# Order of ScalarE's and VectorE's work in the heads of a hybrid decoder block: recurrence work queued behind the takes, weight splits written one product ahead

## The chip, the cores and the metric

The kernel runs on one core of a Trainium2 chip. The metric is the device time of one execution in microseconds (us), as the median of several executions. Before the change it is 1460.81 us (3 runs, 1459.44 to 1462.52).

## The reference

One layer of a decoder block on x of 1024 tokens by 1024 channels, all in float32. Cut to what matters:

```python
proj = x @ w_in                       # 1024 x 7168
q, f_pre, i_val, o_gate, pool_v, gate_a, gate_b = jnp.split(proj, splits, axis=-1)
qf = silu(q) * 128 ** -0.5
f = lb + (1.0 - lb) * sigmoid(f_pre)
k = 1.0 - f
# per head (8 heads of 128): S_t = diag(f_t) S_{t-1} + k_t v_t^T ; o_t = S_t^T q_t
o = hgrn2_chunked(qf, k, i_val, log(f))
o = o * rsqrt(mean(o * o, -1) + 1e-6)             # per head
a = (o * hgrn_norm_g * sigmoid(o_gate)) @ w_a
pooled = causal_multiscale_pool(pool_v)           # trailing means over 2, 4, 8, 16 tokens, minus the token
b = per_group(pooled @ w_pool) * pool_scale
mix = (sigmoid(gate_a) * a + sigmoid(gate_b) * b) @ w_out
x = layer_norm(alpha * x + mix)
x = layer_norm(alpha * x + square(relu(x @ w_up)) @ w_down)
```

## The kernel before, in words

**Products.** A float32 product is made of three float32r matmuls: each operand is split into a high part (a cast on ScalarE, L126 for weights, L131 for activations) and a low part (the rest, a subtraction on VectorE, L127 and L132), and high x high, high x low and low x high are summed in one PSUM bank (`prod`, L212, L214, L215: 12 matmuls of 128x128 by 128x512 for a contraction of 512). A large product is a 2 by 2 block scheme with seven products in place of eight (`pair`, L267): seven weight operands, four of them blocks and three sums of blocks (`make_t3` L284, `make_t2` L301, `t4` L309, `t1` L316, on VectorE), and seven products p1 to p7. Their results are drained by copies on ScalarE (`copied`, L275) and sums on VectorE (`added`, L279), and handed to a "take", which is what this place in the kernel does with the result (a sigmoid, a store). Here these drains and takes together are called takes.

**The heads.** After the value projection (to about 115 us) come 24 such pairs one after the other: inputs of the heads (q and f), output gates, pooled values, gates a and b (`ORDER`, `POOL_AFTER`, L33 to L38). Each pair loads its raw weight blocks on SyncE's DMA queue (`loaded_blocks`, L231). `run` (L379) writes, for each of the seven steps, the weight operand (sum and split), then the product with its takes, and then one "turn" of what goes beside it. In this part TensorE's instructions keep the order in which they are written (`manual_schedule`); the other engines' instructions are put in order by a scheduler which goes by priority (the order of writing, with takes up by 60) and by its own estimate of when things are ready. Each engine then works through its queue in that order, and an instruction that has to wait holds up what stands behind it.

**Beside the products.** `recurrence` (L1046) gives the turns: 16 halves (8 heads by 2 halves of the tokens), 8.25 turns each. A half's `prepare` (L890) makes the scaled queries and keys: scans on VectorE (L897, L901, L905), k = 1 - f on ScalarE (L909), products on VectorE (L935 to L956) and copies of half tiles on ScalarE (L940, L943, L953, L955). `scores`, `far_queries`, `states` and `outputs` follow; `outputs` (L1019) squares the output on ScalarE (L1031), takes the root (L1032, with the load of another activation table), its reciprocal on VectorE (L1033), and scales the output by it in four ScalarE instructions (L1035), all in one turn. In the last two pairs (gates 6 and 7) the turns are those of `pool_products` (L746): weights and pooled rows are loaded, split (L126, L127) and multiplied (`mm3`, L113 to L115), and each result is multiplied on VectorE by a gate that is loaded again from DRAM (`loaded(gbd...)`, L784, L791) into a ring of four tiles, and stored (L792). The last two results are only scaled, on ScalarE (L789).

**What follows.** `o_operand` (L628) loads four tiles of the heads' outputs (L635) and splits them (L131, L132) for the products with w_a; "a11" is the first of seven such operands (L1167). Then come the products with w_a (`a_pair`, L1142; their takes load gates and pooled rows again, L1129, L1130), w_out, the norms and the MLP.

Of the kernel before, what the change touches and what calls it, by code (L numbers as in the profile page):

```python
# [29 lines left out]
PER_HALF = 8.25  # L30
TURN_BACK = 4
TURNS_AHEAD = 3
ORDER = (  # L33
# [18 lines left out]
def tile_hybrid_block(  # L52
# [189 lines left out]
    def w_tile():  # L242
        return wq.tile([P, CH, P], F32R, tag="w", name=nm("w"), bufs=NW)

    def w_part(src):
        return split(src, w_tile)

# [19 lines left out]
    def pair(raw, rooms, takes, pz_tag="pj", twin=False, pc_tag="pj", turned=False):  # L267
# [5 lines left out]
        def copied(room, ps):  # L273
            t = room()
            A.copy(t, ps)  # L275
            return t
# [377 lines left out]
    with tc.tile_pool(name="tmp", bufs=1, side="right", reuse_waits="tile") as tmp:  # L654
# [25 lines left out]
        def head_inputs(h, behind=()):  # L680
            fs, qs = inputs[h] = [None, None], [None, None]

            def room_f():
                fs[1] = tt("f")
                return fs[1]

            def take_f(u):
                def take(src):
                    t = fs[u] = fs[u] or tt("f")
                    A.activation(t, src, AF.Sigmoid)  # L690
                    A.activation(t, t, AF.Identity, bias=lb[:, h : h + 1], scale=one_lb[:, h : h + 1])
                return take

            def take_q(u):
                def take(src):
                    t = qs[u] = tt("q")
                    A.activation(t, src, AF.Sigmoid)
# [5 lines left out]
            run(pair(  # L703
                blocks, (c_soon, c_late, room_f),
                (take_q(0), take_f(0), take_q(1), take_f(1)),
            ), behind=behind)

# [4 lines left out]
        def output_gates(h):  # L712

            def take(dst, src=False):
                def put(t):
                    s = c_late() if src else t
                    A.activation(s, t, AF.Sigmoid)
                    nc.sync.dma_start(out=dst, in_=s)
                return put

            run(pair(
                loaded_blocks(w_in, 3 * D + h * P, 3 * D + (h + 1) * P), (c_soon, c_late, c_late),
                (take(ogd[h][0]), take(ogd[h + 1][0], True), take(ogd[h][1]), take(ogd[h + 1][1])),
            ))

        def gates(j):
# [3 lines left out]
            def take(dst, src=None, u=None):  # L730
                def put(t):
                    s = (tt("og") if final else c_late()) if src else t
                    A.activation(s, t, AF.Sigmoid)
# [5 lines left out]
            run(pair(  # L739
                loaded_blocks(w_in, 5 * D + j * P, 6 * D + j * P), (room if final else c_soon, room, room),  # L740
                (take(gad[j][0]), take(gbd[j][0], True, 0), take(gad[j][1]), take(gbd[j][1], False, 1)),
            ))

        held = [None, None]

        def pool_products():  # L746
# [29 lines left out]
            for n, (g, u) in enumerate(todo):  # L776
# [28 lines left out]
        def pooled(g):  # L805
# [49 lines left out]
            def take_12(ps):  # L855
# [5 lines left out]

            run(pair(
                loaded_blocks(w_in, 4 * D + j * P, 4 * D + (j + 1) * P),
# [21 lines left out]
        class Half:  # L885
# [4 lines left out]
            def prepare(self):  # L890
# [16 lines left out]
                )  # L907
                k = ft
                A.activation(k, ft, AF.Identity, bias=cmask[:, P - 1 : P], scale=-1.0)  # L909
                rT = small("rT", [P, NB])  # L910
# [32 lines left out]
                A.copy(pairs_of(qc)[:, :, 1], pairs_of(q)[:, :, 1])  # L943
                V.tensor_mul(pairs_of(qc)[:, :, 0], pairs_of(q)[:, :, 0], bc(rT2[:, :, 0], [P, NB // 2, SUB]))
# [7 lines left out]
                self.k64 = k64 = hgp.tile([P, CH, 2, 32], F32, tag="k64", name=nm("k64"))  # L952
                A.copy(q64[:, :, 0], half64(q, 1)[:, :, 0])  # L953
                V.tensor_mul(q64[:, :, 1], half64(q, 1)[:, :, 1], bc(p32[:, :, 2], [P, CH, 32]))
                A.copy(k64[:, :, 1], half64(kr, 0)[:, :, 1])  # L955
                V.tensor_mul(k64[:, :, 0], half64(kr, 0)[:, :, 0], bc(p32[:, :, 1], [P, CH, 32]))  # L956
# [62 lines left out]
            def outputs(self):  # L1019
# [13 lines left out]
                V.reciprocal(ss, ss)  # L1033
                for c in range(CH):
                    A.activation(on[:, chunk(c)], o[:, chunk(c)], AF.Copy, scale=ss[:, c : c + 1])  # L1035

# [9 lines left out]
        def recurrence():  # L1046
# [10 lines left out]
            for n in range(2 * HEADS + 1):  # L1057
# [28 lines left out]
        with tc.manual_schedule(engines={mybir.EngineType.PE}):  # L1086
            turns = turning[0] = recurrence()
            output_gates(0)
            for what, j in ORDER:
                if what == "inputs":  # L1090
                    head_inputs(j)
                else:
                    dict(gates=gates, pooled=pooled, output_gates=output_gates)[what](j)
            stream = pool_products()
            next(stream)
            for j, counts in POOL_AFTER.items():
                turning[0] = beside(stream, counts)
                gates(j)
            for _ in turns:
                pass  # L1100
# [65 lines left out]

        o_operand("a11")  # L1167
        for i in range(2):
# [372 lines left out]
```

## Time and profile before

| what | us |
|---|---|
| median of the runs | 1460.81 |
| the profiled execution's own time | 1460.42 |
| its span, from the first to the last instruction | 1458.7 |
| TensorE busy in the span | 1433.3 |
| VectorE busy | 1100.4 |
| ScalarE busy | 759.3 |
| GpSimd busy | 106.7 |

TensorE is busy for 98% of the span. In the rows, a group is named by line, engine and tiles (out<-in). "Idle before" is the time in which the instruction's engine had nothing to do just before it, and the arrow names what ended that. SPq is SyncE's queue, whose instructions issue DMAs.

### The profile page before, as it was taken

To read this page: it belongs to the slowest core of one execution; us is meant where nothing else is said; L and a number is where in the kernel's file an instruction comes from. 1 tells how busy PE (TensorE), PEld (TensorE's weight loads), DVE (VectorE), ACT (ScalarE), POOL (GpSimd) and SP (SyncE) were. 2 spreads that over 40 slices of the span, in tenths; PEclk is the share of its full clock that TensorE was granted. 3 is DMA by queue.
4 is the path that set the end of the run, shared out by engine and by line. 5 is a ranking of instruction groups with operands and counts; after the bars stand their busy time and mean duration, and the time that the engine had idled before them with its cause. 6 is when DMAs were issued, how large, how long until landed. Compare 5 with 4: busy or idle time off the path is not lost.

```text
span 1458.7 us, 20882 instructions
## 1 busy us (share of the span) xinstructions
PE 1433.3 (98%) x7377; PEld 1188.7 (81%) x7377; DVE 1100.4 (75%) x1807; ACT 759.3 (52%) x1383; POOL 106.7 (7%) x288
## 2 busy tenths in 40 slices
PE   9999999999999999989999999999999999999997
PEld 7888888888887887868888888888888888888886
DVE  6968878888697795579885598666666787777877
ACT  5445567566656655556442366555555443333535
POOL 0002112112212110000002100000000100000000
PEclk9999999999999999999999999999999999999999
DMA  7242344444454455689463125444447774445322
GB/s 267 65 130 88 99 125 138 123 112 143 110 133 127 123 132 169 192 315 354 135 231 111 68 92 188 158 144 154 146 162 262 281 253 156 148 141 171 121 73 115
DMA packets 187161, 228.15 MB, mean 156 GB/s; under 512 B 12176, under 2 KB 110512, under 8 KB 187056
## 3 DMA queue, kind: packets, MB, share of 16 engines
q1 hardware_dynamic: 181088, 212.91, 44.0%
q0 software_dynamic: 5184, 11.54, 4.1%
q10 hardware_dynamic: 784, 2.38, 0.5%
q8 instruction: 58, 0.95, 0.3%
q14 instruction: 47, 0.39, 0.1%
HBM read 149.70 MB, written 77.07 MB: 155 GB/s over the span
## 4 chain that ended last, share of the span: by engine, by line
PE 86%; DVE 7%; DMA 3%; ACT 2%; issue 1%; SPq 0%; DVEq 0%; ACTq 0%
PE ps_pj L212 14%; PE ps_pj L215 14%; PE ps_pj L214 14%; PE ps_pj L1423 4%; PE ps_pj L1424 4%; PE ps_pj L1422 4%; PE ps_pj L114 2%; PE ps_pj L115 2%; PE ps_pj L113 2%; PE ps_tr L1423 1%; PE ps_tr L1424 1%; PE ps_tr L1422 1%; DVE w L127 1%; PE ps_hg L212 1%; PE ps_sc L215 1%
## 5 line engine op out<-in xcount | busy, mean ns | idle before, releaser
L212 PE MATMUL ps_pj<-act,w 128*128 128x512 f32 x1068 | 422.2, 395 | 12.4 <-ACT c L275 5.6
L215 PE MATMUL ps_pj<-act,w 128*128 128x512 f32 x1068 | 416.7, 391 | 0.6 <-DVE w L127 0.6
L214 PE MATMUL ps_pj<-act,w 128*128 128x512 f32 x1068 | 416.6, 391 | 0.0
L126 ACT CAST w<-raw 128x512 fp32r<-128x512 f32 x311 | 192.9, 622 | 272.0 <-PE ps_pj L214 184.0
L127 DVE TENSOR_TENSOR w<-raw,w 128x512 fp32r<-128x512 f32 x311 | 213.0, 687 | 102.2 <-ACT w L126 100.8
L212 PEld LDWEIGHTS ps_pj<-act,w 128*128 128x128 f32 x1068 | 201.3, 188 | 58.0 <-ACT c L275 7.4
L215 PEld LDWEIGHTS ps_pj<-act,w 128*128 128x128 f32 x1068 | 201.2, 188 | 44.7 <-DVE w L127 1.8
L214 PEld LDWEIGHTS ps_pj<-act,w 128*128 128x128 f32 x1068 | 201.3, 188 | 40.7
L1384 ACT CAST act<-act 128x1024 fp32r<-128x1024 f32 x66 | 66.9, 1050 | 109.0 <-issue 35.0
L1424 PE MATMUL ps_pj<-act,act 128*128 128x512 f32 x240 | 93.0, 389 | 0.0
L1423 PE MATMUL ps_pj<-act,act 128*128 128x512 f32 x240 | 93.0, 389 | 0.0
L1385 DVE TENSOR_TENSOR act<-act,act 128x1024 fp32r<-128x1024 f32 x66 | 79.5, 1221 | 17.8 <-ACT act L1384 17.8
L1422 PE MATMUL ps_pj<-act,act 128*128 128x512 f32 x240 | 92.5, 389 | 0.0
L279 DVE TENSOR_TENSOR c<-c,ps_pj 128x512 f32<-128x512 f32 x91 | 62.1, 682 | 31.0 <-PE ps_pj L215 30.6
L275 ACT COPY c<-ps_pj 128x512 f32<-128x512 f32 x92 | 53.5, 582 | 3.0 <-PE ps_pj L215 1.7
L1422 PEld LDWEIGHTS ps_pj<-act,act 128*128 128x128 f32 x240 | 45.0, 188 | 9.4
L1423 PEld LDWEIGHTS ps_pj<-act,act 128*128 128x128 f32 x240 | 45.0, 188 | 9.4
L1424 PEld LDWEIGHTS ps_pj<-act,act 128*128 128x128 f32 x240 | 45.0, 188 | 9.3
L284 DVE TENSOR_TENSOR raw<-raw,raw 128x512 f32<-128x512 f32 x43 | 29.6, 689 | 30.5 <-DMA raw<-in_w_in_dram 28.6
L1293 ACT ACTIVATE c<-c 128x512 f32<-128x512 f32 x61 | 38.6, 633 | 1.7
L1292 ACT ACTIVATE c<-c 128x512 f32<-128x512 f32 x46 | 29.1, 632 | 15.6 <-DVE c L279 15.5
L1378 DVE TENSOR_TENSOR act<-act,ps_pj 128x512 f32<-128x512 f32 x45 | 30.2, 683 | 5.4 <-PE ps_pj L1424 5.1
(415 smaller groups left out, 2683.5 us busy)
## 6 DMA issues: line engine op xcount, KB each, us to landing
h<-c SPq DMA_DIRECT2D x106, 256.0 KB, 2.8
raw<-in_w_in_dram SPq DMA_DIRECT2D x100, 256.0 KB, 3.1
act<-h SPq DMA_DIRECT2D x78, 256.0 KB, 3.0
draw<-in_w_down_dram SPq DMA_DIRECT2D x16, 1024.0 KB, 7.8
raw<-in_w_up_dram SPq DMA_DIRECT2D x56, 256.0 KB, 2.9
hf<-h SPq DMA_DIRECT2D x34, 256.0 KB, 2.9
s<-og POOLq DMA_DIRECT2D x28, 256.0 KB, 6.2
v<-v SPq DMA_DIRECT2D x16, 256.0 KB, 3.2
```

What stands on the lines that cost most here:

```text
L126: A.copy(hi, src)
L127: V.tensor_sub(lo, src, f(hi))
L212: PE.matmul(ps, wh[:, k], th, start=first and k == 0, stop=False, skip_group_check=True)
L214: PE.matmul(ps, wh[:, k], tl, start=False, stop=False, skip_group_check=True)
L215: PE.matmul(ps, wl[:, k], th, start=False, stop=k == CH - 1, skip_group_check=True)
L275: A.copy(t, ps)
L279: V.tensor_add(t, t, ps)
L1384: A.copy(hi, src)
L1385: V.tensor_sub(lo, src, f(hi))
L1422: PE.matmul(ps, hh[:, w], wh, start=fresh and n == 0, stop=False, skip_group_check=True)
L1423: PE.matmul(ps, hh[:, w], wl, start=False, stop=False, skip_group_check=True)
L1424: PE.matmul(ps, hl[:, w], wh, start=False, stop=n == M - 1, skip_group_check=True)
```

## The change

It has four parts, all of which move instructions and add or remove none:

1. *ScalarE's recurrence work behind takes.* The take's ScalarE instruction is noted (`noted`), and k = 1 - f, the half-tile copies of `prepare` and the four scalings are written with `behind_act()`: on ScalarE's queue they stand behind the take noted last. k = 1 - f moves one piece later in `prepare`; the scalings move out of `outputs` into `scale_outputs`, one turn later (`TURN_SCALE`).
2. *Weights ahead.* `run_ahead` writes the operand of step n + 1 (its sum and split) ahead of product n and its takes, across pairs too. It takes the place of `run` for all pairs of the heads but the first.
3. *Pool operands behind weights.* The splits of `pool_products` stand behind the last weight's split on ScalarE and VectorE.
4. *The first operand of the next stage.* The loads of `o_operand("a11")` stand behind the last gate load on SyncE's queue, and its splits behind the split of the fourth weight from the end.

`tc.issue_after(i)` queues what the block writes on i's engine behind i; it is an order and no wait.

```diff
+TURN_SCALE = 1
...
     def w_part(src):
-        return split(src, w_tile)
+        hi, lo = w_tile(), w_tile()
+        hi_of.append(A.copy(hi, src).ins)
+        lo_of.append(V.tensor_sub(lo, src, f(hi)).ins)
+        return hi, lo
+
+    @contextmanager
+    def behind_weight(n=-1):
+        with tc.issue_after(hi_of[n]), tc.issue_after(lo_of[n]):
+            yield
+
+    def noted(i):
+        last_act[0] = i.ins
+        return i
+
+    def behind_act():
+        return tc.issue_after(last_act[0])
...
         def copied(room, ps):
             t = room()
-            A.copy(t, ps)
+            noted(A.copy(t, ps))
             return t
...
+    pending = []
+
+    def finish_pending():
+        while pending:
+            pending.pop(0)()
+
+    def run_ahead(steps):
+        for (operand,), ((_, product),) in steps:
+            w = operand()
+            finish_pending()
+
+            def product_and_turn(product=product, w=w):
+                product(w)
+                next(turning[0], None)
+
+            pending.append(product_and_turn)
...
             def parts(g, u, raw, pods):
-                if raw is not None:
-                    w_parts[g] = split(raw, lambda: wide(w_tiles(F32R)))
-                return [split(t, row_tile) for t in pods]
+                with behind_weight():
+                    if raw is not None:
+                        w_parts[g] = split(raw, lambda: wide(w_tiles(F32R)))
+                    return [split(t, row_tile) for t in pods]
...
-                    t = tt("v") if final else loaded(gbd[j][u], lambda: tt("f"))
+                    t = tt("v") if final else tt("f")
+                    if not final:
+                        last_gate[0] = nc.sync.dma_start(out=t, in_=gbd[j][u]).ins
...
-                k = ft
-                A.activation(k, ft, AF.Identity, bias=cmask[:, P - 1 : P], scale=-1.0)
...
                 V.tensor_mul(q, q, fd)
+                k = ft
+                with behind_act():
+                    A.activation(k, ft, AF.Identity, bias=cmask[:, P - 1 : P], scale=-1.0)
                 self.kr = kr = tt("tE")
                 V.tensor_mul(kr, k, to_end)
                 yield
                 self.kc = kc = tt("tD")
-                A.copy(pairs_of(kc)[:, :, 0], pairs_of(kr)[:, :, 0])
+                with behind_act():
+                    A.copy(pairs_of(kc)[:, :, 0], pairs_of(kr)[:, :, 0])
...
-                for c in range(CH):
-                    A.activation(on[:, chunk(c)], o[:, chunk(c)], AF.Copy, scale=ss[:, c : c + 1])
+                self.o, self.root = o, ss
+
+            def scale_outputs(self):
+                with behind_act():
+                    for c in range(CH):
+                        w = chunk(c)
+                        A.activation(self.on[:, w], self.o[:, w], AF.Copy, scale=self.root[:, c : c + 1])
...
                 for turn in range(1, round(at) - round(at - PER_HALF)):
+                    if turn == TURN_SCALE and old:
+                        old.scale_outputs()
                     if turn == TURN_BACK:
...
+            finish_pending()
             stream = pool_products()
             next(stream)
             for j, counts in POOL_AFTER.items():
                 turning[0] = beside(stream, counts)
                 gates(j)
+                finish_pending()
...
-        o_operand("a11")
+        with tc.issue_after(last_gate[0]), behind_weight(-4):
+            o_operand("a11")
```

The other three half-tile copies (L943, L953, L955) get `behind_act()` in the same way, the sigmoids of the takes get `noted(...)`, and `head_inputs` (but for head 0), `output_gates`, `gates` and `pooled` call `run_ahead` in place of `run`.

More of the change, by code (lines that the diff above doesn't have):

```diff
@@ L702, in head_inputs @@
                 blocks = loaded_blocks(w_in, h * P, D + h * P)
-            run(pair(
+            steps = pair(
                 blocks, (c_soon, c_late, room_f),
                 (take_q(0), take_f(0), take_q(1), take_f(1)),
-            ), behind=behind)
+            )
+            if h:
+                run_ahead(steps)
+            else:
+                run(steps, behind=behind)
         def values(h, u):
@@ L716, in put @@
                     s = c_late() if src else t
-                    A.activation(s, t, AF.Sigmoid)
+                    noted(A.activation(s, t, AF.Sigmoid))
                     nc.sync.dma_start(out=dst, in_=s)
                 return put
-            run(pair(
+            run_ahead(pair(
                 loaded_blocks(w_in, 3 * D + h * P, 3 * D + (h + 1) * P), (c_soon, c_late, c_late),
@@ L737, in take @@
                 return put
-            run(pair(
+            run_ahead(pair(
                 loaded_blocks(w_in, 5 * D + j * P, 6 * D + j * P), (room if final else c_soon, room, room),
@@ L860, in take_12 @@
                 second(c22, 1)
-            run(pair(
+            run_ahead(pair(
                 loaded_blocks(w_in, 4 * D + j * P, 4 * D + (j + 1) * P),
@@ L952, in prepare @@
                 self.k64 = k64 = hgp.tile([P, CH, 2, 32], F32, tag="k64", name=nm("k64"))
-                A.copy(q64[:, :, 0], half64(q, 1)[:, :, 0])
+                with behind_act():
+                    A.copy(q64[:, :, 0], half64(q, 1)[:, :, 0])
                 V.tensor_mul(q64[:, :, 1], half64(q, 1)[:, :, 1], bc(p32[:, :, 2], [P, CH, 32]))
-                A.copy(k64[:, :, 1], half64(kr, 0)[:, :, 1])
+                with behind_act():
+                    A.copy(k64[:, :, 1], half64(kr, 0)[:, :, 1])
                 V.tensor_mul(k64[:, :, 0], half64(kr, 0)[:, :, 0], bc(p32[:, :, 1], [P, CH, 32]))
@@ L1033, in outputs @@
                 V.reciprocal(ss, ss)
[L1034 to L1035 removed]
+                self.o, self.root = o, ss
+            def scale_outputs(self):
+                with behind_act():
+                    for c in range(CH):
+                        w = chunk(c)
+                        A.activation(self.on[:, w], self.o[:, w], AF.Copy, scale=self.root[:, c : c + 1])
             def turn_outputs(self):
```

11 lines of the change are left out of this document (6 added, 5 removed).

## The prediction

> **What bounds the kernel now.** I read the page first, then what TensorE waits for between 118 and 665 us (the heads), then the rows around its longest waits. On the page, TensorE's busy time and the chain that ended last:
>
> ```profile
> PE 1433.3 (98%) x7377; PEld 1188.7 (81%) x7377; DVE 1100.4 (75%) x1807; ACT 759.3 (52%) x1383; POOL 106.7 (7%) x288
> ...
> PE 86%; DVE 7%; DMA 3%; ACT 2%; issue 1%; SPq 0%; DVEq 0%; ACTq 0%
> ```
>
> TensorE is the bound: 25 us of the 1458.7 us span are not busy. The change touches no matmul, so it can only win TensorE's waits and what they bring. The waits of TensorE in the heads, with total, times and longest:
>
> ```profile
> PE ps_pj L212 <- ACT c L275: 5.4, 2, 3.1
> PE ps_pj L212 <- ACT w L126: 5.3, 1, 5.3
> PE ps_pj L212 <- ACT f L275: 0.8, 1, 0.8
> PE ps_pj L215 <- DVE w L127: 0.6, 2, 0.5
> PE ps_pj L212 <- DVE c L279: 0.6, 1, 0.6
> ```
>
> They sum to 12.7 us in seven waits, half of what TensorE has. Nine tenths of it (11.5) are ScalarE's: a copy out of PSUM or a weight's cast that came late. Here is the first of the two long copies, ScalarE's queue and then TensorE:
>
> ```profile
> 444.76 0.30 ACT L1032 ACTIVATE ss<-ss,eps_rms 128x4 f32<-128x4 f32 x1
> ...
> 445.65 0.72 ACT L909 ACTIVATE f<-f,cmask 128x512 f32<-128x512 f32 x1 [0.59 <-DVE tC L905]
> 446.56 1.14 ACT L1035 ACTIVATE tH<-ps_hg,ss 128x128 f32<-128x128 f32 x4 [0.19 <-DVE ss L1033]
> 448.08 0.61 ACT L275 COPY c<-ps_pj 128x512 f32<-128x512 f32 x1
> ...
> 448.75 0.50 PE L212 MATMUL ps_pj<-act,w 128*128 128x512 f32 x1 [2.24 <-ACT c L275]
> 449.09 0.40 PE L214 MATMUL ps_pj<-act,w 128*128 128x512 f32 x1
> 449.32 0.39 PE L215 MATMUL ps_pj<-act,w 128*128 128x512 f32 x1
> ```
>
> The copy of a finished product (448.08) stands behind k = 1 - f and four scalings, which wait for VectorE's chain; TensorE waits 2.24 us to write that bank again. Two more things are to be seen. A matmul is shown 0.40 long but the next follows after 0.23, so an idle time shown is some 0.16 less than what is lost; and the first after a wait is followed after 0.34, 0.11 more. Each wait thus costs 0.27 more than its row says. The second:
>
> ```profile
> 560.33 0.62 ACT L126 CAST tD<-tC 128x512 fp32r<-128x512 f32 x1 [4.20 <-DMA tC<-in_w_pool_dram]
> ...
> 561.37 0.58 ACT L275 COPY c<-ps_pj 128x512 f32<-128x512 f32 x1
> ...
> 562.00 0.50 PE L212 MATMUL ps_pj<-act,w 128*128 128x512 f32 x1 [3.14 <-ACT c L275]
> ...
> 564.36 0.63 PE L214 MATMUL ps_pj<-act,w 128*128 128x512 f32 x1
> 564.78 0.63 PE L215 MATMUL ps_pj<-act,w 128*128 128x512 f32 x1
> ...
> 562.00:566.50 4.50, 4.50 (x13) 3.56 (x14) 2.86 (x5) 2.77 (x4) 0.00 (x0) 0.62 0.25 75
> ```
>
> A pool weight's split, not needed for tens of us, waits 4.20 us for its load at the head of ScalarE's queue, the copy behind it. After this wait matmuls follow at 0.42 in place of 0.23: the granted clock (0.62 in the last row, third from its end) is low for 4.5 us, which costs (1 - 0.62) x 4.5 = 1.7 us more. The longest wait, SyncE's, ScalarE's, VectorE's and TensorE's rows:
>
> ```profile
> 635.50 0.73 SPq L635 DMA_DIRECT2D c<-o  x1
> ...
> 640.46 0.62 ACT L131 CAST act<-c 128x512 fp32r<-128x512 f32 x1 [7.80 <-DMA c<-o]
> 640.98 0.61 ACT L126 CAST w<-raw 128x512 fp32r<-128x512 f32 x1
> ...
> 641.11 0.69 DVE L132 TENSOR_TENSOR act<-c,act 128x512 fp32r<-128x512 f32 x1 [5.23 <-ACT act L131]
> ...
> 641.65 0.80 PE L212 MATMUL ps_pj<-act,w 128*128 128x512 f32 x1 [5.27 <-ACT w L126]
> ...
> 642.00:645.50 3.50, 3.50 (x10) 2.63 (x10) 3.47 (x6) 2.26 (x6) 0.00 (x0) 0.59 1.05 397
> ```
>
> The split of the next stage's first operand a11 waits for its load, and the weight that TensorE wants stands behind it; VectorE idles too. Here the clock costs (1 - 0.59) x 3.5 = 1.4 us.
>
> **The change, part by part.** No instruction comes or goes on any engine; TensorE's order is the same up to where the products with w_a begin. So every term is a wait that goes, comes or moves.
>
> *Takes ahead of recurrence work on ScalarE.* In the changed order, the copy of 448.08 stands right behind the root and one weight's split; the root ended at 445.06, split and copy take about 1.1 (0.53 and 0.61), so it is done at 446.2, and TensorE wanted it at 448.75 - 2.24 = 446.5. The wait goes. The wait of 0.8 (f, L275) has the same form and its copy moves up by six instructions: it goes. At 561.37 the pool weight's split now stands 31 instructions behind the copy: the wait of 3.14 goes and the low clock with it. What is late next is the recurrence itself, below. Won: 5.4 + 0.8 + 3 x 0.27 + 1.7 = 8.7 us (7.0 if the clock would be low without it).
>
> On the clock: the Trainium skill ("TensorE: Matmul & The Clock Gate", Part 1) says that the clock falls to half after an idle window of about 3.4 us and comes back after as long a busy one, and that the window runs freely. Here an idle time of 3.14 us was enough and one of 2.24 was not. By that rule the 1.7 us would be in some executions only, since 3.14 is shorter than a window, and the sum of the heads would be 7.0 in the others.
>
> *What that makes late: VectorE.* Behind the copies of `prepare` on ScalarE, VectorE waits with the products that write over what they read (L946, L947), and behind these stand L949, L956, L995 and then the scores on TensorE. In the changed order all of that stands some 10 to 35 VectorE instructions later, and where it now stands takes stand behind it. Whether that costs depends on VectorE's free time (third figure pair of these windows) and on the tail's length:
>
> ```profile
> 400.00:425.00 25.00, 24.45 (x173) 20.19 (x172) 24.97 (x58) 14.29 (x34) 4.13 (x15) 1.00 0.35 96
> ...
> 450.00:475.00 25.00, 25.00 (x176) 21.16 (x175) 18.48 (x37) 14.95 (x36) 4.60 (x14) 1.00 0.51 139
> ...
> 525.00:550.00 25.00, 25.00 (x170) 20.83 (x169) 24.97 (x59) 15.37 (x36) 5.59 (x14) 1.00 0.51 127
> ```
>
> ```profile
> 449.44 0.42 DVE L947 TENSOR_TENSOR tE<-tE,T 128x256 f32<-128x256 f32 x1
> ...
> 400.69 0.68 DVE L949 TENSOR_TENSOR tC<-tE,ek 128x512 f32<-128x512 f32 x1
> ...
> 404.17 0.68 DVE L279 TENSOR_TENSOR c<-c,ps_pj 128x512 f32<-128x512 f32 x1
> ```
>
> In the two stretches beside pooled pairs VectorE is busy for 24.97 of 25 us; elsewhere it has a quarter of its time free. The sum of 404.17 is the one TensorE already waits for (the 0.6 above), and in the changed order a tail of about 1.5 us (L947, a sum of weights, L949 and smaller ones) is put right ahead of it. A sum is due one product, 12 x 0.23 = 2.7 us, after its own. I take 1 us for each of the two full stretches: the tail less a third for what slack there is; the other halves, with a quarter of VectorE free, nothing. Bounds: 0, and 1.1 (L947 and L949) in each of 16 halves, 17.6 us. I take 2.0, near the rows of the full stretches.
>
> The scores have room: the last half-tile copy now stands behind the take of 461.44, and TensorE's matmuls of that turn begin at 466.33:
>
> ```profile
> 461.44 0.58 ACT L275 COPY c<-ps_pj 128x512 f32<-128x512 f32 x1
> ...
> 466.33 0.38 PE L1025 MATMUL ps_hg<-v,att 128*128 128x128 f32 x2
> ```
>
> some 4 us after it, so 0.
>
> *Weights a product ahead.* The sums and casts hardly move among themselves: a weight's cast already waits for its buffer in the ring of ten. So I take nothing beside the above; that a sum comes ahead of a take, or the reverse, is within VectorE's bounds. The raw loads of the heads keep their places on SyncE's queue within two, so nothing.
>
> *a11 behind the last gate load.* In the changed order the weight of 640.98 stands ahead of the a11 splits, and the wait of 5.27 goes from there. But the load of 635.50 now stands behind the last gate load, and the scaling of the first of the last two pool results, which TensorE needs to get one of two banks back, stands five places behind the first a11 split:
>
> ```profile
> 649.50 0.42 SPq L623 DMA_DIRECT2D f<-gb  x1
> ...
> 653.98 0.69 ACT L789 ACTIVATE v<-ps_tr,prm 128x512 f32<-128x512 f32 x1
> ...
> 657.87 0.40 PE L113 MATMUL ps_tr<-w,tF 128*128 128x512 f32 x1
> ```
>
> By the clock of before, the load would go at 649.6 and land 4.9 later (640.46 - 635.50), at 654.5; the five instructions between add 2.6 (0.52 each, 640.46 to 640.98), so the scaling would begin at 657.1 in place of 653.98 and end at 657.8. Since VectorE's idle 5.23 goes, the chain of gates may run up to that much earlier: 652.6. What goes from TensorE is 5.27 + 0.27 + 1.4 and the two waits for w L127 (0.6 + 0.54): 8.1 us. Without them TensorE comes to the matmul that needs the bank at 657.87 - 8.1 = 649.8, and waits 2.8 to 8.0 there. So 0.1 to 5.3 are won. I take 1.0, near the late end: the load's 4.9 stays whole, and a wait of over 3 us brings the low clock back, as at 562.
>
> *Later loads in the next stage.* Eleven loads of L635 were issued ahead of 649.50; now they come behind it. With them eleven low parts of 0.6 us on VectorE (start to start) move into the stretch after 660, where it is fuller:
>
> ```profile
> 660.00:750.00 90.00, 90.00 (x399) 74.51 (x398) 77.50 (x125) 44.02 (x79) 0.00 (x0) 1.00 0.69 225
> ...
> 743.70 0.68 DVE L279 TENSOR_TENSOR room<-room,ps_pj 128x512 f32<-128x512 f32 x1
> ...
> 745.22 0.39 PE L212 MATMUL ps_pj<-act,w 128*128 128x512 f32 x1
> ```
>
> VectorE has 12.5 us free in 90. At 745.22 a product begins 0.84 us after the sum that it needs (743.70 + 0.68): the nearest miss of the stage. If the loads and VectorE's work come later by more than that against TensorE, TensorE waits. Bounds: 0, and 11 x 0.6 = 6.6. I take 3.0, just under the middle.
>
> **Sum.** 8.7 - 2.0 + 1.0 - 3.0 = 4.7 us won. Against the execution's own time of 1460.42 that is 1455.7; this is 0.4 under the median of the runs, so beside it 1456.1. I give 1456.0.
>
> **Rivals.**
>
> *The pool wait shrinks as well.* If the gate loads run by VectorE's whole 5.23 us earlier, 5.3 are won there and not 1.0, and the wait left (2.8) is too short for the low clock. For it: that idle time is VectorE's alone; against it: the a11 load lies behind all gate loads. Time: 1456.0 - 4.3 = 1451.7.
>
> *Nothing is left of it.* What is won in the heads is waited for at 745.22, where the order of loads sets the time and not TensorE; or the scheduler's order is another on the chip than its estimate and the takes stay late. For it: 0.84 us of room; against: VectorE's 12.5 free us. Time: 1460.4, with a us or two to either side.
>
> *Slower: VectorE becomes the bound of the heads.* The tails are put ahead of takes in each of the 16 halves. If VectorE is behind in most, not two, each costs about its 1.1 us: 13 x 1.1 + 3.0 (loads) - 8.7 - 1.0 = 7.6 us lost, 1468; with nine such halves 3.2, 1463.6. It decides from seven halves on (7.7 + 3.0 - 9.7 = 1.0 lost). For it: 24.97 of 25 in two stretches; against: 18.48 of 25 in one like most.
>
> **Chances and range.** Forecast 0.55, with a range of its own of 1452 to 1460; pool wait shrinks 0.13; nothing left 0.18; slower 0.14. A measurement of this kernel can tell about 0.2%, 2.9 us, from no change: faster is below 1457.9, slower above 1463.7. Of the forecast, 0.45 is faster and 0.10 the same; so faster 0.58, same 0.28, slower 0.14. The range for 8 in 10 takes in the pool rival with 1.7 below it and the slower one up to nine halves: 1450 to 1464.
>
> **What would show it.** Right: no wait of L212 for ACT c or f of L275 above 1 us in the heads, no low clock near 562, ScalarE's casts of pool weights behind takes; new waits for DVE c L279 of about 1 us, beside pooled pairs; one wait of 4 to 6 us in the last pool products, for the scaling (L789 of before) and not for a weight; a wait of 1 to 3 us before the norms begin. Wrong: waits for DVE c in most halves (the slower rival), a pool wait under 3 us (the faster one), or TensorE's waits for scores.

## The result, and the profile after

The changed kernel takes 1449.52 us (median of 4, 1448.50 to 1449.96) against 1461.66 for the kernel before (median of 4, the three earlier ones among them): the ratio is 0.9918, with a 95% interval of 0.9901 to 0.9935. That is 12.1 us won; 4.7 were forecast, and the time lies half a microsecond below the range. The profiled execution took 1449.96, its span is 1448.2, 10.5 less than before. The page after, busy times and the chain that ended last:

```profile
PE 1429.7 (99%) x7377; PEld 1187.4 (82%) x7377; DVE 1100.0 (76%) x1807; ACT 757.6 (52%) x1383; POOL 104.0 (7%) x288
...
PE 90%; DVE 5%; DMA 3%; ACT 1%; issue 1%; SPq 0%; DVEq 0%; ACTq 0%
```

TensorE is still the bound, with 18.5 us of the span not busy in place of 25. All waits of TensorE between 118 and 668 us, after (total, times, longest):

```profile
PE ps_tr L114 <- ACT v L833: 2.9, 1, 2.9
PE ps_pj L213 <- DVE c L298: 1.9, 2, 1.0
```

The table of before had 12.7 us in five rows. No wait for a copy (c or f of L275, now L294) is left, nor one for a weight; VectorE's waits grew from 0.6 to 1.9, and a wait for the scaling of a pool result (L789, now L833) came. Here is the first long copy again, on ScalarE:

```profile
443.87 0.58 ACT L294 COPY c<-ps_pj 128x512 f32<-128x512 f32 x1
445.10 1.14 ACT L1090 ACTIVATE tH<-ps_hg,ss 128x128 f32<-128x128 f32 x4 [0.65 <-DVE ss L1082]
446.11 0.64 ACT L250 CAST w<-raw 128x512 fp32r<-128x512 f32 x1
```

The copy that ran at 448.08, behind k = 1 - f and four scalings, now runs at 443.87 with the scalings behind it. Near 561 the copy now runs at 554.66, with scalings behind it, and the pool weight's split, which stood ahead of it, runs at 580.83 without a wait for its load. ScalarE's rows come first; the row of windows then has the clock (third figure from the end) full where it was 0.62:

```profile
554.66 0.58 ACT L294 COPY c<-ps_pj 128x512 f32<-128x512 f32 x1
555.14 1.14 ACT L1090 ACTIVATE tH<-ps_hg,ss 128x128 f32<-128x128 f32 x4
...
580.83 0.65 ACT L127 CAST tD<-tC 128x512 fp32r<-128x512 f32 x1
```

```profile
557.00:561.00 4.00, 4.00 (x20) 3.30 (x19) 3.18 (x5) 3.38 (x5) 0.00 (x0) 1.00 0.02 8
```

The two places where VectorE now holds TensorE:

```profile
404.79 0.50 PE L213 MATMUL ps_pj<-act,w 128*128 128x512 f32 x1 [0.95 <-DVE c L298]
...
545.17 0.50 PE L213 MATMUL ps_pj<-act,w 128*128 128x512 f32 x1 [0.97 <-DVE c L298]
```

The pool products, with the last two gate loads (f) and the first a11 loads (c) on SyncE's queue, then ScalarE and TensorE; behind them the row of windows with the clock:

```profile
635.63 0.90 SPq L828 DMA_DIRECT2D f<-gb  x2
636.58 0.90 SPq L672 DMA_DIRECT2D c<-o  x2
...
642.07 1.31 ACT L132 CAST act<-c 128x512 fp32r<-128x512 f32 x2 [6.83 <-DMA c<-o]
643.29 0.61 ACT L127 CAST w<-st 128x512 fp32r<-128x512 f32 x1
643.82 0.58 ACT L294 COPY q<-ps_pj 128x512 f32<-128x512 f32 x1
644.68 0.62 ACT L132 CAST act<-c 128x512 fp32r<-128x512 f32 x1 [0.29 <-DMA c<-o]
645.21 0.68 ACT L833 ACTIVATE v<-ps_tr,prm 128x512 f32<-128x512 f32 x1
...
645.94 0.50 PE L114 MATMUL ps_tr<-w,tF 128*128 128x512 f32 x1 [2.87 <-ACT v L833]
```

```profile
645.90:650.20 4.30, 4.26 (x12) 3.39 (x13) 3.90 (x8) 4.30 (x9) 0.00 (x0) 0.60 0.99 339
```

This is the moved wait in the form that the prediction gave it: ScalarE waits 6.83 us for the a11 load, the scaling stands behind three a11 splits, and TensorE waits 2.87 for the bank, with the low clock behind it. Its size is not the forecast's: 4 to 6 us was the sign of the forecast, under 3 that of the rival in which the pool wait shrinks as well.

TensorE's order is the same in both kernels up to 668 us, so each matmul's start can be held against its own start before; how much earlier it starts is called its lead. That gives the account of the 10.5 us. Lead won: 0.9 at the wait of 309, 2.5 at 448, 0.4 at 476, 5.1 at 562 (3.15, and 1.95 while the clock had been low), 7.8 from the wait at 641 to 650. Lead lost: 0.4 at 404, 1.1 at 545, 2.9 at the scaling and 1.6 in the low clock behind it; 0.4 more went at the start, at loads of x that the change doesn't touch. Sum 10.3; behind 668 nothing is lost, and up to 770 TensorE has no wait there in either kernel. The medians differ by 1.7 more: the profiled execution of before lies 1.2 under the median beside which it stands now, that of after 0.4 above its own.

### The profile page after: what moved, and what is told of

Read it like the earlier page. It is cut to its first block, busy times and chain, and to the rows that moved or that the text cites. A ratio compares the mean times of both kernels' runs of the same rounds, so it can differ in the third digit from the quotient of the medians.

```text
span 1448.2 us, 20889 instructions
## 1 busy us (share of the span) xinstructions
PE 1429.7 (99%) x7377; PEld 1187.4 (82%) x7377; DVE 1100.0 (76%) x1807; ACT 757.6 (52%) x1383; POOL 104.0 (7%) x288
## 4 chain that ended last, share of the span: by engine, by line
PE 90%; DVE 5%; DMA 3%; ACT 1%; issue 1%; SPq 0%; DVEq 0%; ACTq 0%
PE ps_pj L213 15%; PE ps_pj L215 15%; PE ps_pj L216 15%; PE ps_pj L1484 4%; PE ps_pj L1482 4%; PE ps_pj L1483 4%; PE ps_pj L116 2%; PE ps_pj L115 2%; PE ps_pj L114 2%; PE ps_tr L1484 1%; PE ps_tr L1482 1%; PE ps_tr L1483 1%; PE ps_hg L215 1%; PE ps_sc L213 1%; PE ps_sc L215 1%; PE ps_hg L213 1%
## 5 line engine op out<-in xcount | busy, mean ns | idle before, releaser
L250 ACT CAST w<-raw 128x512 fp32r<-128x512 f32 x303 | 187.6, 622 | 270.3 <-PE ps_pj L215 191.1
L251 DVE TENSOR_TENSOR w<-raw,w 128x512 fp32r<-128x512 f32 x303 | 206.9, 686 | 98.6 <-ACT w L250 96.3
L294 ACT COPY c<-ps_pj 128x512 f32<-128x512 f32 x92 | 53.5, 581 | 3.7 <-PE ps_pj L216 2.2
```

Of the source, the lines that this page charges most:

```text
L250: hi_of.append(A.copy(hi, src).ins)
L251: lo_of.append(V.tensor_sub(lo, src, f(hi)).ins)
L294: noted(A.copy(t, ps))
```

## The experiments

Each time is a median, beside the kernel before in the same set of runs (1461.31, 1461.28, 1462.73 and 1461.58 in the four sets). Ratios are to the kernel before, and runs of different sets are compared by their ratios where it matters. The parts are numbered as in the section on the change: 1 takes, 2 weights ahead, 3 pool splits, 4 a11.

### Is it the fourth part that took the wait near 641 away?

*Parts 1, 2 and 3, without the fourth.*

```diff
-        with tc.issue_after(last_gate[0]), behind_weight(-4):
-            o_operand("a11")
+        o_operand("a11")
```

> The changed kernel without its fourth part: loads and splits of a11 are placed by priority, as before. Theory A (the moved wait is worth what the trace says): the wait for the weight behind the first a11 split comes back with its low clock (5.27 + 0.27 + 1.4 and the small waits for w, 7.8 of lead in the trace), and the 2.9 for the scaling with its low clock (4.5 in all) goes: 3.3 us slower than the changed kernel, 1452.8. Theory B (as predicted, the later loads cost the next stage 3.0 and only the pool wait was mis-sized): the loads come earlier again, so 3.0 come back there: 1449.8. Rival C: the fourth part does nothing, since the heads alone make room: 1449.5, with no wait for a weight in the pool products.

Measured: 1449.71, ratio 0.9920 (0.9902 to 0.9938), the same as the changed kernel. The long wait for a weight did not come back. The first a11 split still waits on ScalarE, as before; TensorE's waits are others:

```profile
629.78 0.62 ACT L132 CAST act<-c 128x512 fp32r<-128x512 f32 x1 [4.65 <-DMA c<-o]
```

```profile
PE ps_tr L114 <- DVE f L835: 2.9, 4, 1.3
PE ps_pj L213 <- DVE c L298: 2.4, 3, 1.0
PE sc L1031 <- ACT k L1004: 0.6, 1, 0.6
```

Four waits for gated results of 2.9 us in all, with no low clock, stand where the changed kernel has one of 2.87 with it. By its time rival C was right; but room in the heads is not the reason: with the first and the third part and neither of the others the wait is there again, as a set below shows.

*The fourth part alone, put into the kernel before.*

```diff
-        o_operand("a11")
+        with tc.issue_after(last_gate[0]), behind_weight(-4):
+            o_operand("a11")
```

> The kernel before with the fourth part alone. Theory A (the wait near 641 has two covers, either of which is enough: weights a product ahead, or the a11 splits behind the weights): the wait of 5.27 for a weight goes, a wait of 3 to 5 us for the scaling comes with a low clock, and the waits near 448 and 561 stay: 3 us won, 1457 to 1458. Rival B (as predicted, 8.1 won and 7.1 given back at the scaling, and 3.0 more lost in the next stage): 1461 to 1463. Rival C (the first theory after the result: the fourth part is what took the wait away, and it needs the second for it): the weight waits still, 1461.

Measured: 1462.25, ratio 0.9999 (0.9985 to 1.0013). Waits in the heads and the pool products:

```profile
PE ps_pj L212 <- ACT c L287: 4.7, 2, 2.6
PE ps_pj L212 <- DVE c L291: 2.8, 2, 2.2
PE ps_tr L113 <- DVE f L805: 2.7, 2, 2.0
PE ps_tr L113 <- ACT v L803: 2.4, 1, 2.4
PE ps_pj L212 <- ACT f L287: 0.4, 1, 0.4
```

The wait for the weight is gone, as theory A said, but its time is not won: 2.7 us for gated results and 2.4 for the scaling take its place, with a low clock behind the longest of each. (The wait of 2.2 for VectorE's sum, near 505, is new as well and has a low clock behind it, but it is no effect of the part: every engine's order is that of the kernel before up to 608 us.) In this respect the prediction was right (what goes at the weight is paid again at the scaling); its sum for this part, 1.0 won and 3.0 lost, is at the edge of what the interval leaves open (1.9 lost).

### Is the second part worth nothing?

*The changed kernel without the second part* (`run` in place of `run_ahead` everywhere).

```diff
-            run_ahead(pair(
+            run(pair(
```

> The changed kernel without its second part: each weight's sum and split is written right ahead of its own product, as before; takes, pool splits and a11 as in the changed kernel. Theory A (a weight that is written one product ahead is the cover under which a wait at the head of ScalarE's queue no longer reaches TensorE): waits for w come back where ScalarE waits for a load in the pool products, 3 to 5 us: 1453 to 1455. Rival B (as predicted, the second part is worth nothing beside the others): 1449.5, the same two waits for c near 404 and 545 and one of 2.9 for the scaling.

Measured: 1453.00, ratio 0.9940 (0.9926 to 0.9955), 3.5 slower. The intervals of the two ratios just overlap; the times themselves do not (1450.96 to 1454.02 here, 1447.19 to 1450.61 in nine executions of the changed kernel). No wait for a weight came: 2.0 for gated results, 1.7 for the scaling, and 1.5 for the scores, which the prediction had put at 0 and the changed kernel does not have. Theory A was right in size and wrong in form. The profiled execution (1450.96) is the fastest of its six, and its trace shows 1.0 of the 3.5; the rest isn't shown.

*The second part alone, put into the kernel before.*

```diff
+    def run_ahead(steps):
+        for (operand,), ((_, product),) in steps:
+            w = operand()
+            finish_pending()
...
-            run(pair(
+            run_ahead(pair(
```

> The kernel before with the second part alone. Theory A (weights ahead cover the wait for the a11 load): the wait of 5.27 for a weight near 641, its low clock and the two small ones for w go, 7.8 of lead, and waits for gates of 3 to 4 us come in their place; the two copies near 448 and 561 stay late: 1457. Rival B (the second part is worth nothing by itself): 1461, with all of the waits of before. Rival C (with the weights ahead, all drains are late and the copies wait longer): above 1462.

Measured: 1456.85, ratio 0.9973 (0.9958 to 0.9988), as theory A said. ScalarE, and TensorE while ScalarE waits:

```profile
629.05 0.62 ACT L126 CAST w<-raw 128x512 fp32r<-128x512 f32 x1 [0.95 <-PE ps_tr L114]
...
636.62 0.62 ACT L131 CAST act<-c 128x512 fp32r<-128x512 f32 x1 [5.72 <-DMA c<-o]
...
635.07 0.40 PE L115 MATMUL ps_tr<-w,tE 128*128 128x512 f32 x1
635.30 0.40 PE L212 MATMUL ps_pj<-act,w 128*128 128x512 f32 x1
635.53 0.39 PE L214 MATMUL ps_pj<-act,w 128*128 128x512 f32 x1
```

The a11 split waits 5.72 us at the head of ScalarE's queue, and TensorE goes from pool products (L115) to the next weight's product (L212) at 635.30 with no idle time: that weight was cast at 629.05, ahead of the split. In the kernel before it was cast at 640.98, behind it. Most of the lead that this wins is paid again: it goes from 0.8 us at 626 to 7.9 at 645 and is 2.6 at 668, as 4.3 us of waits for gated results come, the last with a low clock.

*Parts 1 and 3, with neither the second nor the fourth.* Both edits above that take a part out of the changed kernel.

> The changed kernel without its second and fourth part, so that neither cover of the a11 load is there. Theory A (either was enough, so without both the wait is back): a wait of some 5 us for a weight (ACT w) near 635 with a low clock, 7.8 in all, where the changed kernel has 4.5: 1452.8; the heads' waits for copies stay gone. Rival B (takes and pool splits alone make room for it): no wait for w over 1 us, 1449.5 or less.

Measured: 1452.43, ratio 0.9941 (0.9927 to 0.9956). All waits of TensorE in the heads and the pool products:

```profile
PE ps_pj L213 <- ACT w L250: 5.0, 1, 5.0
PE ps_pj L213 <- DVE c L298: 2.0, 2, 1.1
```

Theory A: the wait for the weight is back. So the a11 load's wait reaches TensorE through the weight only where neither part is there. Either cover is enough, and only the second one wins time: with parts 1 and 3 already in (ratio 0.9941), adding the second gives 0.9920, 3.1 us less, and adding the fourth 0.9940, no difference.

### Do later a11 loads and splits cost the next stage?

*The a11 splits as in the changed kernel, the loads not behind the last gate load.*

```diff
-        with tc.issue_after(last_gate[0]), behind_weight(-4):
+        with behind_weight(-4):
```

> The changed kernel with the a11 splits behind the fourth weight from the end, but its loads not behind the last gate load: on SyncE's queue they stand ahead of the last gate loads, the first two about 10 us earlier. Theory A (the 2.87 wait of TensorE is the latency of the first a11 load in front of the scaling, and nothing else is late): the wait and its low clock go, 4.5 to 4.8 us: 1445. Rival B (the eleven loads on SyncE's queue ahead of gate loads hold these up, or a ring of tiles does): the wait moves to a gate load or stays, 1449 to 1453. Rival C (late loads cost the next stage 3.0, as predicted): beyond 4.8 another 3, 1442.

Measured: 1447.29, ratio 0.9906 (0.9888 to 0.9923), 2.2 under the changed kernel. The wait for the scaling is gone, and its load's wait on ScalarE with it; 0.9 for a gated result and 0.7 for a copy at 727 came. So the wait was the load's latency, as theory A had it, but only half of what it cost is won, where theory A had all of it (1445).

*Splits behind the last scaling.*

```diff
-        with tc.issue_after(last_gate[0]), behind_weight(-4):
+        with tc.issue_after(last_gate[0]), tc.issue_after(last_scale[0]), tc.issue_after(lo_of[-1]):
             o_operand("a11")
...
-                        A.activation(t, ps, AF.Copy, scale=pscale[:, j : j + 1])
+                        last_scale[0] = A.activation(t, ps, AF.Copy, scale=pscale[:, j : j + 1]).ins
```

> The changed kernel with the a11 splits behind the last scaling of the pool products on ScalarE and behind the last weight on VectorE; loads behind the last gate load as in the changed kernel. Loads and splits are later than in any other order. Theory A (the later work has room in the next stage): the wait of 2.87 and its low clock go, nothing comes: 1445. Rival B (the prediction's step: later splits and loads cost the next stage up to 6.6, 3.0 as taken): 1448 to 1451, with waits for VectorE's sums or for act between 655 and 760 us.

Measured: 1450.01, ratio 0.9925 (0.9908 to 0.9943). The wait for the scaling is gone here too, 5.0 us of lead on the changed kernel at 650; by 667 it is 1.1. VectorE, and the row of windows with TensorE's clock:

```profile
650.14 3.09 DVE L133 TENSOR_TENSOR act<-c,act 128x512 fp32r<-128x512 f32 x5
653.15 0.68 DVE L298 TENSOR_TENSOR q<-q,ps_pj 128x512 f32<-128x512 f32 x1
```

```profile
653.88:658.38 4.50, 4.50 (x13) 3.54 (x14) 4.50 (x8) 2.79 (x6) 0.00 (x0) 0.62 0.76 284
```

Five low parts of a11 and its successor (3.09 us) stand ahead of a sum that TensorE needs (653.15): it waits 1.98 there, and the clock is low behind that. This is the prediction's step on later loads, with a price of 3.9, where the splits are later still (rival B). In the changed kernel, the same stretch:

```profile
650.00:740.00 90.00, 90.00 (x399) 74.49 (x398) 81.65 (x134) 47.84 (x85) 0.00 (x0) 1.00 0.74 246
```

VectorE is busy for 81.65 of 90 us there, where it was for 77.50 before, and TensorE for all 90 at the full clock. The work moved in, and the room held it.

### What are the first and the third part worth?

*The first part alone* (behind_act and noted as in the change; `run`, pool splits and a11 as before), and a second time.

```diff
+                with behind_act():
+                    A.activation(k, ft, AF.Identity, bias=cmask[:, P - 1 : P], scale=-1.0)
...
-            A.copy(t, ps)
+            noted(A.copy(t, ps))
```

> The first part alone: ScalarE's recurrence work behind takes, weights, pool splits and a11 as before. Theory A: the waits at 309 and 448 go (0.94 and 2.5 of lead), the one near 562 stays with its clock, since a pool weight's split and not recurrence work stands ahead of that copy, and the one near 641 stays; VectorE gives back 1.5: 1459. Rival B (the copy near 561 is a take too and stands ahead of the split once takes are queued first): 5.1 more, 1454. Rival C (VectorE's later tail costs in most halves without the weights ahead): 1462 or more.

Measured: 1453.68, ratio 0.9952 (0.9935 to 0.9968).

> The first part alone, a second time, as its profiled execution (1457.98) lay 4 us above the median of its executions (1453.68). Theory A (the wait of 5.49 for the weight near 639 is there in each execution and the 4 us are elsewhere: small ones at the start and in waits for transfers): median 1453.5, the wait over 5 us again, the wait near 560 with or without a low clock. Rival B (the wait for the a11 load is itself a matter of chance): the wait near 639 under 3 us in an execution of 1453 to 1454.

Measured: 1455.47, ratio 0.9957 (0.9943 to 0.9972); profiled 1455.96. So 6 to 8 us, more than theory A's 2; it is about the time of the first run's rival B, but not by its way: the copy does not stand ahead of the split, as the rows below show. In both profiled executions the wait near 639 for the weight is there (5.49 and 4.17), and the one near 562 is 1.30 and 1.06 in place of 3.14, with no low clock. New are 1.1 and 1.6 us for the scores, near 494. ScalarE near 560, in the first of the two:

```profile
554.53 0.30 ACT L1080 ACTIVATE ss<-ss,eps_rms 128x4 f32<-128x4 f32 x1
558.57 0.62 ACT L127 CAST tD<-tC 128x512 fp32r<-128x512 f32 x1 [3.74 <-DMA tC<-in_w_pool_dram]
559.09 0.61 ACT L250 CAST w<-raw 128x512 fp32r<-128x512 f32 x1
559.61 0.58 ACT L294 COPY c<-ps_pj 128x512 f32<-128x512 f32 x1
```

The pool weight's split still stands ahead of the copy and waits for its load; the load landed 1.8 us sooner, the wait of TensorE is shorter by that, and no low clock followed. The first profiled execution was 4.3 us above its median and 2.0 above the second one; of the 2.0, 1.0 arose at the start and 1.3 in the wait for the weight, with smaller ones either way, and where the rest of the 4.3 lies isn't shown. In the second, the wait for the weight (4.17) lies between what its theory A (over 5) and its rival B (under 3) had said.

*The changed kernel without the third part.*

```diff
-                with behind_weight():
-                    if raw is not None:
-                        w_parts[g] = split(raw, lambda: wide(w_tiles(F32R)))
-                    return [split(t, row_tile) for t in pods]
+                if raw is not None:
+                    w_parts[g] = split(raw, lambda: wide(w_tiles(F32R)))
+                return [split(t, row_tile) for t in pods]
```

> The changed kernel without its third part: the splits of pooled rows and pool weights are placed by priority, as before. Theory A: the first pool weight's split waits for its load at the head of ScalarE's queue again, the copy behind it: 3.1 us of TensorE near 557 and a low clock of some 4.5 us, 5.1 in all: 1454.6. Rival B (noting takes and writing weights ahead moved the copy ahead of that split already): 1449.5, no wait there. Rival C: the other pool splits get in the way as well, several waits of ScalarE in the pool products: 1457.

Measured: 1453.79, ratio 0.9950 (0.9933 to 0.9968), 4.3 slower. Theory A's size, by other waits: 1.0 for the copy near 559 at the full clock, 2.5 in small ones, and the wait for the scaling 3.9 with 6 us of low clock. Its profiled execution (1455.97) is the slowest of its six.

*The third part alone.* The same lines added to the kernel before.

> The kernel before with the third part alone: pool splits behind weights. Theory A (the pool weight's split at the head of ScalarE's queue is what holds the copy near 561): the 3.14 goes with its low clock, 5.1 in all; 448 and 641 stay: 1456. Rival B (the four scalings are in front of that copy as well, so that it stays late by 1 to 2 us without the low clock): 1457.5. Rival C (nothing: the copy waits for something else): 1461.

Measured: 1458.56, ratio 0.9981 (0.9967 to 0.9994). The wait near 561 is gone with its clock (theory A's mechanism). By the ratio the part is worth 2.8, by the medians 4.2, where theory A said 5. The profiled execution, 1455.42, is the fastest of its twelve; in it the waits near 448 (3.15) and 636 (3.33, for a weight) have a low clock behind them. Near 448 the kernel before, with the same order on every engine up to there, has 2.24 and the full clock.

### VectorE's tail, and the best order

*Half-tile copies of `prepare` by priority again.*

```diff
-                with behind_act():
-                    A.copy(pairs_of(kc)[:, :, 0], pairs_of(kr)[:, :, 0])
+                A.copy(pairs_of(kc)[:, :, 0], pairs_of(kr)[:, :, 0])
```

(and the three others)

> The changed kernel with the four half-tile copies of prepare placed by priority again; k = 1 - f and the four scalings stay behind takes. Theory A (the late half-tile copies put VectorE's tail ahead of the sum near 404 and 545): the two waits for c shrink to the 0.6 and 0 of before, 1.5 us in all: 1448.0, and no copy gets late, as k and the scalings were what held them up. Rival B (VectorE is full there whatever the order): 1449.5 with both waits. Rival C (half-tile copies hold takes up on ScalarE): a wait for ACT c of 1 to 3 us comes, 1451.

Measured: 1447.62, ratio 0.9910 (0.9894 to 0.9926). The wait at 404 shrank to 0.4 and the one at 545 went, as theory A said; one of 1.46 came at 500. Of the 3.5 us between the two traces 0.4 are the heads' and 2.9 those of the wait for the scaling: 1.24 with the full clock, where it was 2.87 with a low one. Copies did not get late. So the half-tile copies set where VectorE holds TensorE in the heads, and hardly for how long: 1.86 us in two waits here, 1.92 in the changed kernel.

*Both edits together: half-tile copies by priority, a11 loads ahead of the last gate loads.*

> The changed kernel with half-tile copies placed by priority and the a11 loads ahead of the last gate loads (both edits of earlier runs, which gave 1447.6 and 1447.3). Theory A (they win different waits, one in the heads and one in the pool products): 1445.5. Rival B (both win the same 4.5 us of the wait for the scaling and its clock): 1447 to 1447.5.

Measured: 1444.54 (1443.73 to 1445.33), ratio 0.9884 (0.9869 to 0.9899), 5 us under the changed kernel and the best order that was run (theory A). What is left of waits in the heads and the pool products:

```profile
PE ps_pj L213 <- DVE c L298: 1.6, 2, 1.2
PE ps_tr L114 <- DVE f L835: 0.4, 1, 0.4
```

*The changed kernel a second time.*

> The changed kernel itself a second time, on the chip of the run beside it: 1449.5 by its first four executions. Theory A (its wait for the scaling near 646 is there in each execution, its low clock in some): 1448 to 1450, a wait of 2 to 3.5 us there. Rival B (the wait depends on the a11 load's time and goes in some executions): 1445 to 1449.5, wait under 1.5 us in the profiled one.

Measured: 1449.12, ratio 0.9918 (0.9899 to 0.9938). The profiled execution has 2.76 for the scaling and the low clock behind it (theory A).

## Why the prediction was wrong, step by step

Held against its own terms, by the account of starts above and by the runs:

- **Takes: 8.7 forecast, 8.9 in the trace.** Right, place by place, the low clock near 562 included (1.7 forecast, 1.95); 0.4 at 476 was not on its list.
- **VectorE gives back: 2.0 forecast, 1.5.** Right: two places, both in the stretches named, of 0.95 and 0.97 shown, and none elsewhere. That the half-tile copies behind takes put the waits at these two places is shown; that without them VectorE would give back less is not, since 1.46 came at 500 in their stead.
- **Weights a product ahead: "I take nothing beside the above". This step failed.** The part alone wins 4.4 by its median (ratio 0.9973, which leaves 1.8 to 6.1), and 3.1 by the ratios beside parts 1 and 3. The prediction looked only at how sums and casts move among themselves. What they move past is other work on ScalarE: a cast written a product earlier stands ahead of a split that waits 5 us for its load, and that wait no longer reaches TensorE. In the trace of the part alone 1.9 us of lead are won by this, behind 626, net of the gated results' waits; the other places that make up the median's 4.4 are not all shown.
- **a11: 1.0 won forecast, 3.2 in the trace (7.77 less 4.54).** The step was mis-sized: for the wait, the near bound (5.3 won, 2.8 us of wait left) was right. The last gate load was issued at 636.21 in place of 649.50, 13.3 us earlier, and TensorE's lead out of the heads is only 7.1 of that; the other 6.2 are what the rival "the pool wait shrinks as well" had said (5.23 by its reckoning). The low clock, which that rival had left out at 2.8 us, came at 2.87 and cost 1.6. And it is not this part that earned it: without it the time is the same (1449.71), alone it is worth 0 (ratio 0.9999).
- **Later loads in the next stage: 3.0 lost forecast, 0.** This step failed. The loads are later against TensorE, as forecast (the load that the first split waits for went at 635.50, behind two others at 608 and 615; now the first of all goes at 636.58, where TensorE is 14.8 us ahead), and VectorE has 4 us more to do between 650 and 740; but none of it reaches TensorE. The prediction took half of its bound from one product with 0.84 us of room; behind 668 TensorE's own order isn't fixed, and it is another in the changed kernel. Whether the free time of VectorE or the other order takes the loads in is not shown. The mechanism exists: with the splits behind the scaling it costs 3.9.

Of the 7.4 us between forecast and result, 3.0 are the later loads, 2.2 the a11 step, 0.7 the first two steps, 1.7 the two profiled executions' places among their own, and 0.4 at the start go the other way; that makes 7.2. The two large ones have one root: the prediction read the times of what was moved from the old trace, at its nearest or late end, though the gate loads that a11 was moved behind would themselves run 6 us earlier than the heads' lead alone makes them, and though a stretch with 12.5 us free could take 6.6 more. That the second part's gain was counted under the fourth did not change the sum, but that was luck: the second part happened to do what the fourth was credited with. It would have changed any advice on which part to keep.

On the clock: in these runs waits of 1.8 to 2.6 us brought it down in six of ten cases, and waits of about 2.2 us both did and did not. The Trainium skill ("TensorE: Matmul & The Clock Gate", Part 1) gives an idle window of about 3.4 us before the clock falls; the runs here don't agree with that length. It also says that the window is free-running; waits of one length with either outcome would fit that, but no run here shows the window itself.

## What to carry to other kernels

In a queue that is worked in order, an instruction that waits for a load costs only as much as what stands behind it is needed soon: writing the next operand one product ahead takes the wait off the path without touching the load. When several edits can remove the same wait, take each one out of the final kernel and put each one alone into the first: here one of four was worth nothing in each of its three settings (alone, beside 1 and 3, beside 1, 2 and 3), though its splits without its loads won some 2 us (1447.29 against 1449.71 in one set). When a queue ahead of a moved instruction is itself freed, work its new times out from the engine that paces it, not from the old trace.

## What the runs showed of the hardware

Over the sixteen profiled executions, TensorE's waits of more than 1 us, from 100 us into the execution on, fall into three groups by the granted clock in the 4.5 us behind them: 19 waits of 1.01 to 1.76 us, none with a low clock; ten of 1.82 to 2.55, six with it (0.62 in all six); ten of 2.76 to 5.49, all with it (0.50 to 0.69). Two such waits in one kernel, the second part alone:

```profile
448.00:453.50 5.50, 5.33 (x16) 4.24 (x17) 4.73 (x11) 3.09 (x9) 0.21 (x2) 0.69 0.17 48
649.00:654.50 5.50, 5.11 (x15) 4.06 (x16) 5.50 (x10) 3.30 (x6) 0.00 (x0) 0.69 1.01 313
```

The waits ahead of these stretches are of 2.28 and 1.82 us, and the clock falls to 0.69 of full over 5.5 us in both; in the kernel before a wait of 2.24 at the same place left it at 1.00. At 0.62 over 4.5 us a low clock costs an estimated (1 - 0.62) x 4.5 = 1.7 us more (1.6 and 1.95 were measured at two places), so by this estimate two waits of 1.5 us are cheaper than one of 3.

The same order can also give other waits. Up to 560 us every engine's order is the same in the kernel before and with the third part alone, yet near 448 one has a wait of 2.24 us and the full clock, the other 3.15 and a low one, 2.6 us of lead in all. With the fourth part alone, in the same order up to 608, a wait of 2.23 with a low clock near 505 costs 3.8, where the kernel before has none. So the account of a single trace can be off by 2 to 4 us with no change of order at all, and what a part is worth is read from the medians.
